# Load sizes and the ScalarE/VectorE split of a streaming log-sum-exp, set by a landing-time model

## The chip, the cores and the metric

The kernel runs on one core of a Trainium2 chip. The metric is the device time of one execution in microseconds (us). The profile's span is about 1.8 us shorter than the time of the same execution: 164.9 against 166.69 us in the first profile of before.

## The reference

```python
def setup_inputs():
    batch, seq, dim = 32, 512, 1024
    return {"x": np.random.randn(batch, seq, dim).astype(np.float32), "axis": -1}

def reference(x, axis):
    x_max = np.max(x, axis=axis, keepdims=True)
    return (x_max.squeeze(axis) + np.log(np.sum(np.exp(x - x_max), axis=axis))).astype(np.float32)
```

There are 16,384 rows of 1,024 floats, 67.1 MB to read and 64 KB to write. Both kernels leave out the maximum: they compute Ln(sum(Exp(x))), which these inputs allow.

## The kernel before

Each of the 128 partitions owns 128 rows. Below, "a row" means one row in every partition: a 128 x 1024 tile, 512 KB. The rows are loaded in blocks into a ring of 50 row slots. Of each block, the first `n_dve` rows get one large Exp on ScalarE and a row sum on VectorE; each other row gets its own Exp on ScalarE with an accumulator that gives the sum.

```python
CHUNKS = [                      # (rows of the load, rows summed by VectorE)
    (12, 4), (14, 4), (16, 4), (16, 9), (16, 11), (12, 8), (10, 6), (8, 5),
    (6, 4), (5, 3), (4, 2), (3, 1), (2, 0), (2, 0), (1, 0),
]
LAST_PARTS = [512, 512]
RING_ROWS = 50
# ... cut ...
    for r, n_dve in CHUNKS:
        if slot + r > RING_ROWS:
            slot = 0
        nc.sync.dma_start(out=ring[:, slot : slot + r], in_=x_v[:, row : row + r])
        if n_dve:
            nc.scalar.activation(out=ring[:, slot : slot + n_dve], in_=ring[:, slot : slot + n_dve], func=Exp)
            nc.vector.reduce_sum(out=sums[:, row : row + n_dve], in_=ring[:, slot : slot + n_dve], axis=AX)
        for j in range(n_dve, r):
            nc.scalar.activation(out=ring[:, slot + j], in_=ring[:, slot + j], func=Exp,
                                 accum_out=sums[:, row + j : row + j + 1])
        slot += r
        row += r
    # ... cut: the last row is loaded and exponentiated in two halves, with sums in `part`;
    #     between the halves: Ln of the 127 finished rows ...
    nc.vector.reduce_sum(out=sums[:, row : row + 1], in_=part, axis=AX)
    nc.scalar.activation(out=res[:, row : row + 1], in_=sums[:, row : row + 1], func=Ln)
    nc.scalar.dma_start(out=out_v, in_=res)
```

A load that reuses slots must wait until the rows that lay there are finished. The framework puts that wait on the load's issue.

The softmax here doesn't subtract the row's maximum and nothing guards it: scores larger than these inputs give would overflow.

## Time and profile before

| | before |
|---|---|
| time, median of the 3 runs before the prediction (166.33 with a fourth, beside the changed kernel) | 166.36 us |
| span of the profiled execution (its time: 166.69 us) | 164.9 us |
| share of the load queue in 16 DMA engines' span | 95.3% |
| ScalarE / VectorE busy | 76% / 41% |
| last load landed; last Ln ended | 159.53; 162.45 us |

Landing times here and below are the last of a load's 16 completion events in the trace, one for each DMA engine. The "spread" of a load is the time from the first of the 16 to the last.

From the page of before: the span, the mean busy tenths of the DMA engines in 40 slices, and the load queue (packets, MB, share of 16 engines' span).

```profile
span 164.9 us, 255 instructions
...
DMA  6998999997997998999899898999999999999940
...
q1 hardware_dynamic: 2448, 67.11, 95.3%
```

The DMA engines work nearly all the time. A 16-row load, 8.39 MB, took 19.5 us from landing to landing, 430 GB/s. The Trainium skill, "DMA: Bandwidth & Descriptors", section Bandwidth, derives a ceiling of 435 GB/s from the fabric, and this stream runs about 1% below it.

Groups of instructions of before (line, engine, operation, shapes, count; busy us, mean ns; idle before it and what ended that):

```profile
L63 DVE TENSOR_REDUCE sums<-ring 128x4 f32<-128x4096 f32 (+8 forms) x12 | 66.9, 5576 | 87.7 <-ACT ring L60 87.7
L60 ACT ACTIVATE ring<-ring 128x4096 f32<-128x4096 f32 (+8 forms) x12 | 54.5, 4539 | 35.8 <-DMA ring<-in_x_dram 35.7
L67 ACT ACTIVATE ring<-ring 128x1024 f32<-128x1024 f32 x66 | 68.7, 1043 | 0.0
```

ScalarE waits for loads (35.7 us), hardly for anything else. Keeping the shapes apart, Exp of 4,096 elements takes 3,614 ns and of 11,264 takes 9,591 ns, so 0.834 ns an element and about 0.2 us fixed; that fits the 186 ns + 0.833 ns an element, for immediate scale and bias, in the Trainium skill, "ScalarE: Activation LUTs", section "What ACT_TABLE_LOAD costs". A row for VectorE therefore costs ScalarE about 0.85 us, a row that ScalarE sums itself 1.04 us from start to start. A row of load takes 1.22 us.

The end of before, from the timeline (start us, duration us, what; in brackets the idle time before it and its releaser):

```profile
160.50 0.63 ACT L84 ACTIVATE ring<-ring 128x512 f32<-128x512 f32 x1
161.01 0.20 ACT L84 ACTIVATION_READ_ACCUMULATOR ring<-ring 128x1 f32 x1
161.11 0.31 ACT L92 ACTIVATE res<-sums 128x127 f32<-128x127 f32 x1
161.31 0.63 ACT L84 ACTIVATE ring<-ring 128x512 f32<-128x512 f32 x1
161.82 0.20 ACT L84 ACTIVATION_READ_ACCUMULATOR ring<-ring 128x1 f32 x1
162.06 0.15 DVE L93 TENSOR_REDUCE sums<-part 128x1 f32<-128x2 f32 x1 [7.48 <-ACT ring L84]
162.25 0.20 ACT L94 ACTIVATE res<-sums 128x1 f32<-128x1 f32 x1 [0.22 <-DVE sums L93]
162.48 0.37 ACTq L95 DMA_DIRECT2D out_dram<-res  x1
```

All data are there at 159.53, yet the first half row's Exp starts at 160.50: ScalarE has a backlog. The last Ln ends 2.9 us after the last landing. This tail is what can be shortened.

### The profile page before, as it was taken

To read this page: it belongs to the slowest core of one execution; us is meant where nothing else is said; L and a number is where in the kernel's file an instruction comes from. 1 tells how busy PE (TensorE), PEld (TensorE's weight loads), DVE (VectorE), ACT (ScalarE), POOL (GpSimd) and SP (SyncE) were. 2 spreads that over 40 slices of the span, in tenths; PEclk is the share of its full clock that TensorE was granted. 3 is DMA by queue.
4 is the path that set the end of the run, shared out by engine and by line. 5 is a ranking of instruction groups with operands and counts; after the bars stand their busy time and mean duration, and the time that the engine had idled before them with its cause. 6 is when DMAs were issued, how large, how long until landed. Compare 5 with 4: busy or idle time off the path is not lost.

```text
span 164.9 us, 255 instructions
## 1 busy us (share of the span) xinstructions
DVE 67.1 (41%) x13; ACT 125.7 (76%) x151; POOL 0.2 (0%) x4
## 2 busy tenths in 40 slices
DVE  0000073005400082000099200999996949788300
ACT  3000699249990799919996299999989999999993
POOL 0000000000000000000000000000000000000000
DMA  6998999997997998999899898999999999999940
GB/s 191 477 477 382 445 445 445 445 445 318 509 461 318 493 511 366 397 509 413 350 509 461 358 453 382 421 437 477 389 437 421 427 423 432 426 411 417 415 187 16
DMA packets 2593, 67.18 MB, mean 407 GB/s; under 512 B 288, under 2 KB 416, under 8 KB 800
## 3 DMA queue, kind: packets, MB, share of 16 engines
q1 hardware_dynamic: 2448, 67.11, 95.3%
q10 hardware_dynamic: 144, 0.07, 0.1%
q14 instruction: 1, 0.01, 0.0%
HBM read 67.11 MB, written 0.07 MB: 407 GB/s over the span
## 4 chain that ended last, share of the span: by engine, by line
DMA 54%; ACT 32%; DVE 8%; another core or an unknown queue 3%; issue 1%; SPq 0%; ACTq 0%
DMA ring<-in_x_dram 54%; ACT ring L60 16%; ACT ring L67 15%; DVE sums L63 8%; ACT ring L84 1%; SPq L58 0%; ACT res L94 0%; ACT res L92 0%; DVE sums L93 0%; ACTq L60 0%; ACTq L92 0%
## 5 line engine op out<-in xcount | busy, mean ns | idle before, releaser
L63 DVE TENSOR_REDUCE sums<-ring 128x4 f32<-128x4096 f32 (+8 forms) x12 | 66.9, 5576 | 87.7 <-ACT ring L60 87.7
L60 ACT ACTIVATE ring<-ring 128x4096 f32<-128x4096 f32 (+8 forms) x12 | 54.5, 4539 | 35.8 <-DMA ring<-in_x_dram 35.7
L67 ACT ACTIVATE ring<-ring 128x1024 f32<-128x1024 f32 x66 | 68.7, 1043 | 0.0
L67 ACT ACTIVATION_READ_ACCUMULATOR ring<-ring 128x1 f32 x66 | 12.5, 190 | 0.0
L93 DVE TENSOR_REDUCE sums<-part 128x1 f32<-128x2 f32 x1 | 0.2, 155 | 7.5 <-ACT ring L84 7.5
L52 ACT ACT_TABLE_LOAD x1 | 1.3, 1283 | 0.7 <-PEq L112 0.7
L84 ACT ACTIVATE ring<-ring 128x512 f32<-128x512 f32 x2 | 1.3, 628 | 0.0
L84 ACT ACTIVATION_READ_ACCUMULATOR ring<-ring 128x1 f32 x2 | 0.4, 202 | 0.0
L94 ACT ACTIVATE res<-sums 128x1 f32<-128x1 f32 x1 | 0.2, 203 | 0.2 <-DVE sums L93 0.2
L92 ACT ACTIVATE res<-sums 128x127 f32<-128x127 f32 x1 | 0.3, 308 | 0.0
L112 POOL MEMSET const-bfloat16-1.0<- 128x1 bf16 x1 | 0.1, 102 | 0.0
L112 POOL MEMSET const-uint8-127<- 128x1 uint8 x1 | 0.1, 102 | 0.0
L112 POOL MEMSET const-float32-0.0<- 128x1 f32 x1 | 0.1, 99 | 0.2 <-issue 0.2
L112 POOL MEMSET const-float32-1.0<- 128x1 f32 x1 | 0.1, 99 | 0.0
## 6 DMA issues: line engine op xcount, KB each, us to landing
ring<-in_x_dram SPq DMA_DIRECT2D x2, 6144.0 KB, 27.4
ring<-in_x_dram SPq DMA_DIRECT2D x1, 7168.0 KB, 33.9
ring<-in_x_dram SPq DMA_DIRECT2D x1, 5120.0 KB, 28.3
ring<-in_x_dram SPq DMA_DIRECT2D x1, 4096.0 KB, 14.7
ring<-in_x_dram SPq DMA_DIRECT2D x1, 3072.0 KB, 21.6
ring<-in_x_dram SPq DMA_DIRECT2D x1, 2560.0 KB, 27.3
ring<-in_x_dram SPq DMA_DIRECT2D x1, 2048.0 KB, 24.1
ring<-in_x_dram SPq DMA_DIRECT2D x2, 1024.0 KB, 30.4
```

What stands on the lines that cost most here:

```text
L52: nc.scalar.preload_act_table_set("natural_log_exp_and_others")
L60: nc.scalar.activation(out=ring[:, slot : slot + n_dve], in_=ring[:, slot : slot + n_dve], func=Exp)
L63: nc.vector.reduce_sum(out=sums[:, row : row + n_dve], in_=ring[:, slot : slot + n_dve], axis=AX)
L67: nc.scalar.activation(out=ring[:, slot + j], in_=ring[:, slot + j], func=Exp, accum_out=sums[:, row + j : row + j + 1],)
L84: nc.scalar.activation(out=ring[:, slot, c : c + w], in_=ring[:, slot, c : c + w], func=Exp, accum_out=part[:, k : k + 1],)
L92: nc.scalar.activation(out=res[:, 0:row], in_=sums[:, 0:row], func=Ln)
L93: nc.vector.reduce_sum(out=sums[:, row : row + 1], in_=part, axis=AX)
L94: nc.scalar.activation(out=res[:, row : row + 1], in_=sums[:, row : row + 1], func=Ln)
L112: nc = _bacc.Bacc("TRN2", target_bir_lowering=False, num_devices=1)
```

## The change

The intent: choose load sizes and splits from a model of when each load lands, so that ScalarE has less backlog at the end; take logs of finished rows between loads; drop the half rows and the last VectorE sum; keep the order of the program (no reordering by the scheduler). The diff, cut to its core:

```diff
 CHUNKS = [
-    (12, 4), (14, 4), (16, 4), (16, 9), (16, 11), (12, 8), (10, 6), (8, 5),
-    (6, 4), (5, 3), (4, 2), (3, 1), (2, 0), (2, 0), (1, 0),
+    (15, 8), (16, 8), (16, 8), (16, 8), (14, 9), (11, 8), (9, 6), (7, 5), (5, 4),
+    (5, 3), (4, 3), (3, 2), (2, 1), (2, 2), (1, 0), (1, 0), (1, 0),
 ]
-LAST_PARTS = [512, 512]
+LN_FROM = 4
 ...
+    ctx.enter_context(tc.manual_schedule())
+    def take_logs(lo, hi):
+        if hi > lo:
+            nc.scalar.activation(out=res[:, lo:hi], in_=sums[:, lo:hi], func=Ln)
 ...
         nc.sync.dma_start(out=ring[:, slot : slot + r], in_=x_v[:, row : row + r])
+        if i == len(CHUNKS) - 1:
+            take_logs(logged, row)
+            logged = row
 ... (Exp and sums of the block as before)
+        if r >= LN_FROM:
+            take_logs(logged, row)     # the rows of the blocks before this one
+            logged = row
 ...
-    (the last row in two halves, VectorE's sum of the two, and its Ln)
+    take_logs(logged, NB)
```

More of the change, by code (lines that the diff above doesn't have):

```diff
@@ L35 @@
     NB = N // P
-    assert sum(r for r, _ in CHUNKS) + 1 == NB and sum(LAST_PARTS) == D
+    assert sum(r for r, _ in CHUNKS) == NB
     fp32 = mybir.dt.float32
@@ L48 @@
     sums = pool.tile([P, NB], fp32, name="sums")
-    part = pool.tile([P, len(LAST_PARTS)], fp32, name="part")
     res = pool.tile([P, NB], fp32, name="res")
     nc.scalar.preload_act_table_set("natural_log_exp_and_others")
-    row = slot = 0
-    for r, n_dve in CHUNKS:
+    ctx.enter_context(tc.manual_schedule())
+    def take_logs(lo, hi):
+        if hi > lo:
+            nc.scalar.activation(out=res[:, lo:hi], in_=sums[:, lo:hi], func=Ln)
+    row = slot = logged = 0
+    for i, (r, n_dve) in enumerate(CHUNKS):
         if slot + r > RING_ROWS:
@@ L72 @@
             )
+        if r >= LN_FROM:
+            take_logs(logged, row)
+            logged = row
         slot += r
         row += r
-    if slot + 1 > RING_ROWS:
-        slot = 0
-    c = 0
-    for k, w in enumerate(LAST_PARTS):
-        nc.sync.dma_start(out=ring[:, slot, c : c + w], in_=x_v[:, row, c : c + w])
-        c += w
-    c = 0
-    for k, w in enumerate(LAST_PARTS):
-        nc.scalar.activation(
-            out=ring[:, slot, c : c + w],
-            in_=ring[:, slot, c : c + w],
-            func=Exp,
-            accum_out=part[:, k : k + 1],
-        )
-        c += w
-        if k == 0:
-            nc.scalar.activation(out=res[:, 0:row], in_=sums[:, 0:row], func=Ln)
-    nc.vector.reduce_sum(out=sums[:, row : row + 1], in_=part, axis=AX)
-    nc.scalar.activation(out=res[:, row : row + 1], in_=sums[:, row : row + 1], func=Ln)
+    take_logs(logged, NB)
     nc.scalar.dma_start(out=out_v, in_=res)
```

## The prediction

> **What bounds the kernel now: the input loads.** The page shows the DMA engines at 9 or 10 tenths in nearly every slice and the load queue at 95.3% of 16 engines' span; ScalarE is busy 76%, VectorE 41%. From what ended ScalarE's waits (timeline) and the queue's semaphore events, the loads land at 18.1, 35.1, 54.7, 74.1, 93.7, 108.2, 120.3, 130.0, 137.3 ... 159.5 us. Between landings each row of 1,024 floats per partition takes 1.21 to 1.23 us, whatever the load's size: a 16-row load took 19.5 us, 430 GB/s. The Trainium skill, "DMA: Bandwidth & Descriptors", section Bandwidth, gives 435 GB/s as the fabric's ceiling; the trace agrees to about 1%. So nothing is left to gain in the middle. ScalarE's idle time (35.7 us in the waits view) all waits for loads.
>
> Only the tail is open: the last load lands at 159.5, the last Ln ends at 162.45, then the store (issue 0.37 us) and completion take 2.4 us to the end, 164.9. A tail without backlog, estimated from trace durations, is 159.5 + 1.2 (one row with its accumulator read) + 0.2 (Ln) + 2.4 = 163.4. So at most about 1.5 us, 0.9%, is to be had.
>
> **What the change does.** It still has 17 loads of the same bytes. First load 15 rows instead of 12: computing starts at about 21.8, not 18.1 (estimate, 1.216 us a row), harmless, since ScalarE idles early on. Rows given to VectorE rise from 61 to 74, each costing ScalarE 0.855 us instead of 1.04 us; that relieves ScalarE by about 2 us over all, mostly where it idles anyway. The final row is one exp, not two halves (0.81 us each to the next), and its Ln follows directly, without VectorE's 2-element sum: 0.2 to 0.4 us saved. Added: 11 more Ln, each about 0.2 to 0.35 us on ScalarE (0.2 from start to start in the trace, plus its wait for ScalarE's own accumulator).
>
> I stepped both programs through by hand with these durations. Before is reproduced to 0.3 us up to the last two half-row loads. After: slots come free in time everywhere. The closest is load 4 (16 rows), which needs load 2's VectorE sum: load 2 lands 41.2, exp to 48.2, sum to 57.0, issue at 57.0, and load 3 lands at 60.7. That is 3.7 us ahead (before: never under 5); the first packet came 1.0 us after the first issue, so I expect no gap. The last load lands at 159.3 to 159.7, as before. In the tail ScalarE is never idle from about 147 on: backlog again, since rows come every 1.22 us but exp, accumulator rows and Ln take nearly that. The last exp starts at about 160.5, held by the 13-row Ln, which waits for VectorE's 2-row sum (ends 160.0 to 160.4). The last Ln ends at 161.9 to 162.0, span about 164.4, against 164.9.
>
> **Prediction: 165.9 us** (166.36 before), range 165.2 to 166.8. Faster by over 2%: 0.01; within 2%: 0.97; slower by over 2%: 0.02.
>
> **What would show it.** Right: landings still 1.22 us a row and the last at 159.3 to 159.7; the fourth load issued near 57 with no dip in GB/s near 59; no ScalarE wait for a load after about 143; the chain ends in ScalarE work and Ln at 161.7 to 162.2. Wrong: a dip after the third load; an Ln waiting over 1 us on VectorE; ScalarE idle before the last load, with the last Ln before 161.3.
>
> **What would make it wrong.** A DMA gap at the fourth load (up to 1 or 2 us longer); Ln costing much more than 0.3 us in order; VectorE sums slower beside ScalarE; single-row loads at the end landing later.

## The result, and the profile after

The changed kernel took 166.43 us (median of 4 runs, 166.17 to 166.64), before 166.33 us (4 runs). Ratios in this document are the mean time of one kernel's fast runs over that of the other's fast runs of the same rounds, so not quite the ratio of the medians; "before" in a ratio is always the kernel before. Here it is 1.0008, 95% interval 0.9989 to 1.0027: no change.

From the page of the changed kernel, the lines that answer to those of before:

```profile
span 164.4 us, 243 instructions
...
DMA  6998999899799979979999989999999999999950
...
q1 hardware_dynamic: 2448, 67.11, 95.2%
```

The stream is as full as it was. The groups of the changed kernel:

```profile
L70 DVE TENSOR_REDUCE sums<-ring 128x8 f32<-128x8192 f32 (+7 forms) x14 | 82.0, 5866 | 78.3 <-ACT ring L67 78.3
L67 ACT ACTIVATE ring<-ring 128x8192 f32<-128x8192 f32 (+7 forms) x14 | 66.8, 4770 | 36.6 <-DMA ring<-in_x_dram 36.5
L74 ACT ACTIVATE ring<-ring 128x1024 f32<-128x1024 f32 x53 | 55.1, 1040 | 0.0
...
L56 ACT ACTIVATE res<-sums 128x16 f32<-128x16 f32 (+8 forms) x12 | 2.4, 198 | 0.4 <-DVE sums L70 0.3
```

Work moved to VectorE as planned (67 to 82 us), and the logs are cheap: 12 of them, 2.4 us busy, and in the timeline 0.10 to 0.16 us from an Ln's start to that of the next Exp.

The chain that ended last in the changed kernel (start us, us, what), from its stretch at the fourth load on:

```profile
48.29 8.70 DVE sums L70
56.98 0.02 issue
57.00 0.33 SPq L62
57.33 0.04 issue
57.37 40.16 DMA ring<-in_x_dram
97.54 0.02 issue
...
142.49 0.02 issue
142.51 2.46 ACT ring L67
...
158.01 2.30 DVE sums L70
...
160.39 0.21 ACT res L56
160.60 1.05 ACT ring L74 x2
161.65 0.02 issue
161.67 0.20 ACT res L56
```

Read it from the bottom. The last Ln ends at 161.87, 2.05 us after the last landing (159.82), where before needed 2.92: the tail did get shorter, by 0.87 us. But the last load landed 0.29 us later than in before's profile, although the bytes and the number of loads are the same. And the third line of the excerpt shows something new: the issue of the fourth load, at 57.00, released by VectorE's sum of the second load, lies 3.7 us before the third load's landing at 60.72. (The chain passes through the issue of the fifth load at 57.37, which waited behind the fourth in the same queue; in before the fourth load was issued at 43.20, 11.5 us ahead.)

The completion events tell where the lateness began. Spread of the 16 engines, load by load, worked out from the trace:

| load | before | changed | changed, second profile (`after_again`, below) |
|---|---|---|---|
| 3 | 0.78 us | 0.89 | 0.95 |
| 4 | 0.78 | 1.45 | 1.64 |
| 5 | 0.88 | 1.41 | 1.61 |
| 10 | 0.78 | 1.42 | 1.60 |
| last | 0.71 | 1.37 | 1.57 |

A load is usable only when its slowest engine is done: the Exp on the fourth load starts at 80.66, 0.03 us after the last of the 16 events. In the changed kernel the slowest engine lost some 0.6 us at the fourth load, and no later load gives that back. In the first profile one engine stood still for at least 0.53 us: the last of the 16 finished its share of the third load at 60.41, and the last first packet of the fourth load began at 60.94. In the second profile no engine stood still, but the first packet took up to 0.78 us longer than the usual 2.44 us. Both were found in the DMA packet records around the boundary, which lie in the packed trace but which no view prints packet by packet. The records do not name the engine, so 0.53 is the least that fits them; the expectation of the second run below says 0.77, which fits another pairing of an end (60.17) with that start.

### The profile page after: what moved, and what is told of

Same layout as the page of the kernel before. It is cut to its first block, busy times and chain, and to the rows that moved or that the text cites. A ratio compares the mean times of both kernels' runs of the same rounds, so it can differ in the third digit from the quotient of the medians.

```text
span 164.4 us, 243 instructions
## 1 busy us (share of the span) xinstructions
DVE 82.0 (50%) x14; ACT 124.2 (76%) x133; POOL 0.2 (0%) x4
## 3 DMA queue, kind: packets, MB, share of 16 engines
q1 hardware_dynamic: 2448, 67.11, 95.2%
## 4 chain that ended last, share of the span: by engine, by line
DMA 65%; ACT 18%; DVE 13%; issue 1%; SPq 0%; ACTq 0%
DMA ring<-in_x_dram 65%; ACT ring L67 14%; DVE sums L70 13%; ACT ring L74 4%; SPq L62 0%; ACT res L56 0%; ACTq L56 0%
## 5 line engine op out<-in xcount | busy, mean ns | idle before, releaser
L70 DVE TENSOR_REDUCE sums<-ring 128x8 f32<-128x8192 f32 (+7 forms) x14 | 82.0, 5866 | 78.3 <-ACT ring L67 78.3
L67 ACT ACTIVATE ring<-ring 128x8192 f32<-128x8192 f32 (+7 forms) x14 | 66.8, 4770 | 36.6 <-DMA ring<-in_x_dram 36.5
L74 ACT ACTIVATE ring<-ring 128x1024 f32<-128x1024 f32 x53 | 55.1, 1040 | 0.0
L74 ACT ACTIVATION_READ_ACCUMULATOR ring<-ring 128x1 f32 x53 | 9.9, 187 | 0.0
L56 ACT ACTIVATE res<-sums 128x16 f32<-128x16 f32 (+8 forms) x12 | 2.4, 198 | 0.4 <-DVE sums L70 0.3
```

Of the source, the lines that this page charges most:

```text
L56: nc.scalar.activation(out=res[:, lo:hi], in_=sums[:, lo:hi], func=Ln)
```

## The experiments

Two theories stood against each other. **H**: the fourth load is issued too late; some DMA engines run short of work for a moment, and every later landing, and the end, come later by that. **Rival**: the stall is chance, and the change gains nothing for another reason (added logs, or an end that DMA and completion alone set). **T** is about the tail: the gain comes from the splits of the last small loads.

All runs were timed in 5 rounds and gave correct results. `before_again`, `after_again`, `swap_early` and `late_issue` ran in one call, `dose_56`, `old_sizes`, `no_mid_logs` and `best_tail` in a second, `dose_18` and `dose_113` in a third, each call on another chip. "Lead" is the landing of the third load less the issue of the fourth, in the profile.

### Both kernels again

No edit.

> The kernel before, unchanged, against itself. It sizes the noise and tells whether the profile of before that the prediction rested on (span 164.9 us in a run of 166.69 us) was typical. Theory A (that profile came from a slowish run; before's usual span is its time less 1.78, about 164.55): ratio 1.000 within 0.002, span 164.4 to 164.7, last load landing at 159.1 to 159.4. Rival (164.9 is the usual span, and the time outside the span varies between the two kernels): span 164.9 again with a time near 166.35.

Measured: 166.45 us, ratio 1.0003 (0.9991 to 1.0015), profiled span 164.6 us in a run of 166.40. The last Ln ended at 162.16, 2.89 us after the last landing. So theory A holds: the first profile of before was of a slowish run. The 11 runs of before in the same rounds had spans of 164.5 to 164.8, median 164.6.

> The changed kernel, unchanged. In its first profile one of the 16 DMA engines stood still for 0.77 us at 60.9 us, when the fourth load began, and from then on the spread between the first and the last engine's landing was 1.4 us instead of 0.9. Theory H (the hole comes from the fourth load being issued only 3.7 us before the third one landed): the hole, of 0.3 to 1.2 us on one or more engines, is there again at 60 to 61 us, and the spread again jumps at the fourth load. Rival (a chance stall): no hole there, spread 0.8 to 1.0 throughout, span 0.3 to 0.5 us shorter. Ratio to before 1.000 within 0.002 in either case.

Measured: 166.52 us, ratio 1.0011 (0.9998 to 1.0024), span 164.5. The spread jumped from 0.95 to 1.64 us at the fourth load again. The expected hole was not there as such; the lateness came as first packets that took too long. That is a partial miss in form, while the place and the size repeat.

### The fourth load issued early, by a swap of sizes

```diff
-    (15, 8), (16, 8), (16, 8), (16, 8), (14, 9), ...
+    (16, 8), (16, 8), (16, 8), (15, 8), (14, 9), ...
```

Now the fourth load fits into the first load's slots and need not wait for the second.

> The changed kernel with the first and the fourth load swapped in size (16 and 15 rows instead of 15 and 16), so that the fourth load needs slots of the first load alone and is issued near 39 us, some 23 us ahead. All else, the tail too, is the same. Theory H: no hole at the fourth load, spread of landings 0.8 to 1.0 to the end, last landing 0.3 to 0.5 us earlier than in the changed kernel, time 0.2 to 0.5 us shorter (ratio to before about 0.998). Rival (chance): the same time as the changed kernel, within 0.1 us.

Measured: issue at 39.07, lead 22.8 us; no engine waited at the fourth load; spread 1.04 us at the third, 1.14 at the fourth, 1.12 at the last load; last landing 159.44. Time 165.71 us, ratio 0.9962 (0.9949 to 0.9975), against 1.0011 of the changed kernel on the same chip. That is 0.8 us from swapping two numbers, more than the 0.2 to 0.5 us expected. The rival (same time) falls. So does another suspect, the fifth load: here it was issued only 3.5 us before the third landing (58.39 against 61.90; in the changed kernel 3.4, 57.37 against 60.72), and nothing was lost.

### The fourth load issued later still

```diff
-    (15, 8), (16, 8), (16, 8), ...
+    (15, 8), (16, 10), (16, 8), ...
```

> The changed kernel with the second load split 10 and 6 instead of 8 and 8, so that VectorE's sum of it ends later and the fourth load is issued at about 61.1 us instead of 57.0, after the third load's landing near 60.7. A dose of the suspected cause. Theory H: all 16 DMA engines stand still for 1.5 to 3 us, all later landings shift by as much, and the time grows by 1.3 to 3 us (ratio 1.008 to 1.018). Rival (the queue has slack, time is set by ScalarE's tail alone): under 0.5 us longer.

Measured: 169.01 us, ratio 1.0149 (1.0136 to 1.0162). The chain of this run, at the same place:

```profile
50.56 10.83 DVE sums L70
61.40 0.02 issue
61.41 0.33 SPq L62
```

And the windows of this run, 59 to 62 us (window, its length, busy us of DVE, ACT and POOL with counts, clock, DMA share, GB/s; DMA share and bytes are booked where a packet starts, and a packet here lasts 2.4 us, so single windows jump about and a share can pass 1):

```profile
59.00:60.00 1.00, 1.00 (x1) 0.00 (x0) 0.00 (x0) 1.00 0.00 0
60.00:61.00 1.00, 1.00 (x1) 0.00 (x0) 0.00 (x0) 1.00 0.01 0
61.00:62.00 1.00, 0.39 (x1) 0.85 (x1) 0.00 (x0) 1.00 0.00 0
```

No load packet starts in these 3 us. The packet records show why the loss is larger than the lateness of the issue. First packets began at 62.37 to 62.76 us, 0.96 to 1.35 us after the issue, and each of the 16 took 0.67 to 1.21 us over its usual 2.44. The fourth load landed at 83.78, 22.4 us after its issue. One caution: in this profile 11 packets in the middle of the second load (started 35.3 to 36.1 us) also took 0.4 to 0.7 us over, with no issue near, and the third load landed at 61.13 where the other profiles with the same first three loads have 60.5 to 60.7. So slow packets also come by chance. What ties the loss to the lead is that it follows the dose and repeats, not the packets of one profile.

### A little earlier, sizes untouched

```diff
-    (15, 8), (16, 8), (16, 8), ...
+    (15, 8), (16, 7), (16, 8), ...
```

> The changed kernel with the second load split 7 and 9 instead of 8 and 8, sizes of the loads unchanged, so that the fourth load is issued at about 55.1 us: some 5.6 us before the third one lands, instead of 3.7. Theory H (the lead of the fourth load's issue is what counts, not the sizes of the first loads): no engine waits at the fourth load's start and no first packet takes much over its usual 2.44 us, spread of landings stays at 0.9 to 1.2 us, time about that of the swapped version: 165.6 to 165.9 us, ratio to before 0.995 to 0.998. Rival (the swap helped through its 16-row first load or by chance): as the changed kernel, ratio 1.000 to 1.002.

Measured: issue at 55.03, lead 5.6 us, spread 0.84 us at the fourth load and 0.80 at the last. Time 165.67 us (165.62 to 165.69), ratio 0.9951 (0.9939 to 0.9963). One row of 128 given to ScalarE instead of VectorE took 0.8 to 0.9 us off the changed kernel. So neither the 16-row first load nor chance made the swap faster; the lead did. The same windows, for comparison with the late run:

```profile
59.00:60.00 1.00, 0.00 (x0) 0.00 (x0) 0.00 (x0) 1.00 1.67 721
60.00:61.00 1.00, 0.00 (x0) 0.35 (x1) 0.00 (x0) 1.00 0.76 328
61.00:62.00 1.00, 0.00 (x0) 1.00 (x1) 0.00 (x0) 1.00 0.76 328
```

How the lateness travels shows in two lines of the timeline: the Exp that starts when the fourth load lands, and the last Exp of the run that waits for a load (the tenth). First the changed kernel, then this run.

```profile
80.66 7.03 ACT L67 ACTIVATE ring<-ring 128x8192 f32<-128x8192 f32 x1 [4.46 <-DMA ring<-in_x_dram]
...
142.51 2.76 ACT L67 ACTIVATE ring<-ring 128x3072 f32<-128x3072 f32 x1 [0.91 <-DMA ring<-in_x_dram]
```

```profile
80.07 7.03 ACT L67 ACTIVATE ring<-ring 128x8192 f32<-128x8192 f32 x1 [3.96 <-DMA ring<-in_x_dram]
...
141.97 2.76 ACT L67 ACTIVATE ring<-ring 128x3072 f32<-128x3072 f32 x1 [0.91 <-DMA ring<-in_x_dram]
```

The fourth landing is 0.59 us earlier, the tenth 0.54 us, and the last Ln ends at 161.32 instead of 161.87, 0.55 us earlier. After 142 us ScalarE is never idle for a load again, so the tenth landing sets the end.

### Two more doses

```diff
+    (15, 8), (16, 9), (16, 8), ...      # dose_18
+    (15, 8), (16, 4), (16, 8), ...      # dose_113
```

> The changed kernel with the second load split 9 and 7: the fourth load issued near 59.0 us, about 1.8 us before the third one lands. In the late run (issue 61.41) the fourth load landed 22.4 us after its issue. Theory H with that number: the fourth load lands at 81.2 to 81.6 instead of 80.2 to 80.8, most engines show a hole or a long first packet, last landing 160.3 to 161.0, time 166.6 to 167.2, ratio to before 1.001 to 1.006: between the changed kernel (lead 3.7, 1.001) and the late run (lead below 0, 1.015). Rival (only an issue after the queue has run empty hurts): as the changed kernel or faster, ratio 0.995 to 1.001.

> The changed kernel with the second load split 4 and 12: the fourth load issued near 49.3 us, about 11.5 us ahead. Theory H (past some lead between 3.7 and 5.6 us more brings nothing): as the run with lead 5.6, ratio to before 0.994 to 0.997, spread of landings 0.8 to 1.2 us. Rival (each microsecond of lead counts, or the split of the second load itself does): another 0.3 us or more faster than that run, ratio below 0.993.

Measured: the first was issued at 58.97, and its fourth load landed at 81.11 (expected 81.2 to 81.6). If the 16 ends of the third load's packets and the 16 starts of the fourth's are paired in order of time, every engine paused, for 0.69 to 1.04 us, and 11 of the 16 first packets took 0.4 to 1.0 us over. It took 166.67 us, ratio 1.0020 (1.0007 to 1.0034). Its time cannot be told from the changed kernel's (1.0011, 0.9998 to 1.0024), but it is clearly slower than dose_56. It was issued before the first engine ran out (59.23), so a load issued while data are still streaming can be too late, and the rival ("only an empty queue hurts") falls. The second was issued at 49.26 and took 165.70 us, ratio 0.9968 (0.9955 to 0.9980): more lead than 5.6 us brings nothing more. Together:

| run | lead | third to fourth landing | ratio to before |
|---|---|---|---|
| dose_113 | 11.2 us | 19.6 us | 0.9968 |
| dose_56 | 5.6 | 19.4 | 0.9951 |
| changed (two profiles) | 3.7, 3.6 | 19.9, 20.2 | 1.0008, 1.0011 |
| dose_18 | 1.6 | 20.5 | 1.0020 |
| late_issue | -0.3 | 22.7 | 1.0149 |

The runs of before add a point between 3.7 and 5.6: their eighth load (8 rows) was issued 5.0 us before the seventh landed, and landed 9.7 us after it, the usual 1.21 us a row, with no growth of the spread (0.77 in the first profile, 0.97 in the second).

### Structure without sizes

The changed kernel with the loads and splits of before (the last row whole, 16 loads):

```diff
+    (12, 4), (14, 4), (16, 4), (16, 9), (16, 11), (12, 8), (10, 6), (8, 5),
+    (6, 4), (5, 3), (4, 2), (3, 1), (2, 0), (2, 0), (1, 0), (1, 0),
```

> The changed kernel's structure (program order kept, logs between loads, one whole last row, no sum on VectorE at the end) with the load sizes and splits of before, 16 loads. Theory T (the tail gains because the last small loads give rows to VectorE, so ScalarE's backlog at the end is shorter; structure alone gives nothing): ScalarE still ends late, last Ln ending near 162.2, span 164.5 to 164.9, ratio to before 0.999 to 1.003. Rival (the gain seen in the swapped version comes from dropping the half rows and the last VectorE sum): ratio 0.996 to 0.998.

Measured: 166.17 us, ratio 0.9983 (0.9971 to 0.9996). This falls between what T and its rival said. The chain's end:

```profile
153.45 4.94 ACT ring L74 x9
...
160.97 1.05 ACT ring L74 x2
162.01 0.02 issue
162.04 0.20 ACT res L56
```

ScalarE still drains rows one by one. The last Ln ends at 162.24, 2.66 us after the last landing: 0.23 less than in the repeat of before (2.89), and 0.61 more than with the new sizes (2.05). So both parts gain in the tail, the sizes more: T was right about the larger part, wrong that the structure gives nothing. In time, of the same rounds, structure gives 0.3 us (0.9983) and the sizes 0.5 us more (dose_56, 0.9951).

### Without the logs between loads

The swapped version with `LN_FROM = 99`: one Ln of 127 columns before the last Exp.

> The swapped version without the logs between the loads: one Ln of 127 columns before the last exp, one of the last column. Theory: an Ln in the stream costs ScalarE 0.10 to 0.16 us from start to start, only two of them lie behind ScalarE's last idle time (142 us), and the longer Ln takes 0.1 us more; so within 0.15 us of the swapped version, ratio to before 0.994 to 0.998. Rival (the added Ln cost the changed kernel its gain): 0.5 us or more faster than the swapped version.

Measured: 165.79 us, ratio 0.9959 (0.9947 to 0.9971); the swapped version had 0.9962. The logs between loads neither cost nor gain anything measurable.

### A shorter tail

Swapped first loads, more and smaller late loads, the last row in halves again, but with the two partial sums meeting in the last Ln, one as its bias, instead of a VectorE sum:

```diff
+    (16, 8), (16, 8), (16, 8), (15, 8), (14, 9), (9, 4), (8, 3), (8, 4),
+    (6, 4), (5, 3), (4, 3), (3, 3), (2, 0), (2, 2), (1, 0), (1, 1), (1, 0),
 ...
+    (two half-row loads; two Exps with accum_out=part[:, 0:1] and part[:, 1:2])
+    nc.scalar.activation(out=res[:, row : row + 1], in_=part[:, 1:2], func=Ln, bias=part[:, 0:1])
```

> Swapped first loads, a tail of loads of 9, 8, 8, 6, 5, 4, 3, 2, 2, 1, 1, 1 rows and two half rows, whose partial sums meet in the last Ln (one as its bias). By the same stepping as in the prediction: ScalarE without idle time from about 145.9, the last exp (half a row) after the last landing near 159.7, last Ln ends at about 161.1, span 163.4 to 163.9, time 165.1 to 165.7, ratio to before 0.993 to 0.996. If the end is set by DMA and completion alone (rival), the same as the swapped version, 165.7.

Measured: 165.57 us, ratio 0.9946 (0.9935 to 0.9958). The last Ln ends at 160.90, 1.56 us after the last landing, 0.5 us less than in dose_56. But the span is only 0.25 us shorter (163.60 against 163.84), since 2.70 us follow the last Ln instead of 2.52, which no run here explains. Its ratio cannot be told from that of dose_56 (0.9951). The median of no_mid_logs was 165.79 and that of dose_56 165.67, against 165.57 with single runs from 165.37 to 165.75; so what a tail shorter than that of dose_56 still pays stays open. Both are faster than both kernels, by about half a per cent.

## Why the prediction was right or wrong

The time, 166.43 us, lies in the range (165.2 to 166.8), and "within 2%" at 0.97 was right. The centre, 165.9, was 0.5 us too low, and how it was reached holds one wrong step, one wrong comparison and errors in the other direction.

- **What bounds the kernel: right.** The landings kept 1.22 us a row but for the fourth (19.91 us for 16 rows, 1.24 a row), and at most about 1.5 us was open in the tail. For that fourth load the last landing, 159.82 and 159.95 in the two profiles, missed the 159.3 to 159.7 that was expected; the versions with more lead had 159.3 to 159.4. No version got more than 0.9 us of it.
- **"3.7 us ahead ... the first packet came 1.0 us after the first issue, so I expect no gap": the step that failed.** It took the first packet of the first engine as the time that a load needs to get going. Already in the first profile of before the last of the 16 engines had its first packet at 2.56, 1.8 us after that issue, and in the late run 1.35 us passed until the last one started, with packets that then took up to 1.21 us over. And engines need new work before the landing: the third load's last packets ended at 59.5 to 60.4 us in the changed kernel, landing at 60.72. What was assumed not to exist, a loss at the fourth load, was 0.55 to 0.71 us (the fourth load landed at 80.63 and 80.75 us, against 80.04 and 80.08 in dose_56 and dose_113). How it arises is not shown. It is not a simple sum of those delays: in the first profile of the changed kernel the engines that ran out first, at 59.5 us and 2.5 us after the issue, went on without a pause, and the losses fell on engines that ran out 3 us or more after the issue. The runs put the necessary lead above 3.7 and at most at 5.6 us (5.0 was enough for an 8-row load of before). The prediction did name this as the first way to be wrong, but gave it no weight in the centre.
- **"A ScalarE backlog again": right**, with VectorE's 2-row sum holding the 13-row Ln as said; it ended at 160.31 (160.0 to 160.4 expected), and the Ln waited 0.34 us. The last Ln ended at 161.87 (161.9 to 162.0 expected) and the span was 164.4, as put. That agreement is partly luck: the tenth load landed at 142.49, 0.54 us later than in dose_56, which has the same loads without the loss, and an Ln cost 0.10 to 0.16 us instead of the 0.2 to 0.35 that were reckoned.
- **"164.4, against 164.9": the wrong comparison.** The span of 164.9 was that of a run of 166.69 us, while the time to be changed was 166.36. The usual span of before is about 164.6. A predicted span of 164.4 meant a time of 164.4 + 1.8 = 166.2, not 165.9. This is 0.3 of the 0.5 us; the rest is that the profiled run, at 166.17, was the fastest of the four.
- **"At about 21.8 ... harmless": right for the first load alone.** But the larger first loads, 15 + 16 + 16 = 47 of 50 slots, and the 8-row VectorE share of the second made the fourth load depend on work that ends at 57.0.

So a gain existed and was given back. With the lead mended the changed kernel is 0.5 to 0.8 us faster than before (dose_113 0.9968, swap_early 0.9962, dose_56 0.9951); the late fourth load costs the changed kernel about that amount. In the profiles the lateness accounts for 0.55 us (161.32 against 161.87), the medians differ by about 0.85 (dose_56) or 0.8 (swap_early); both profiles of the changed kernel fell on its faster runs (166.17 and 166.31 us). Why one engine in particular falls behind, and why its first packet came as late as 3.9 us after the issue in one profile, stays open: the records do not name the engines.

## What to carry to other kernels

In a load stream that never pauses, a model of landing times must also hold the issue times: for each load compare when its slots come free with when the load ahead of it lands, and keep several microseconds between (here 5.0 and 5.6 us were enough, 3.7 was not). The loss hides from the busy share of the DMA engines (95.3% before, 95.2% changed). Look at the time from landing to landing per row, for the lateness stays in every load that follows. The spread between the first and the last completion shows it only when some engines are late and others not: where all were late, it stayed at 0.83 us (dose_18) and 1.00 us (late_issue). And before costing a gain of some tenths of a per cent against a profile, check that the profiled run is a typical one.

## What the Trainium skill lacked or had wrong

- "DMA: Bandwidth & Descriptors", section "Latency and other measured facts", gives about 600 ns to the first byte. The first load here agrees for the first engine (issue ended at 1.10 us, first packet at 1.73), but the page has no figure for the last of the 16 engines (2.56 us in that load) or for the slow first packets: 0.96 to 1.35 us after the issue and 0.67 to 1.21 us over in the late run. It also lacks how far ahead a load must be issued to keep the engines fed: more than 3.7 us, 5.6 us being enough, for loads of 64 KB a partition (5.0 us for one of 32 KB).
- The same page, section Bandwidth, has one sentence by which the HBM side, about 358 GB/s, binds transfers between HBM and SBUF. It wants a condition: the same section measures 425 GB/s for one core and gives about 358 for each of two cores that stream together. This load stream on one core ran at 430 GB/s.
- No page that was read has it that a lateness of some DMA engines persists from load to load: a spread of 1.45 us at the fourth load was still 1.37 us at the seventeenth.
